# A one-core hybrid decoder layer: w_o's sums moved into the last branch, four transfers of x, and other orders on VectorE

## The chip, the cores and the metric

The kernel runs on one core of a Trainium2 chip. The engines that matter are TensorE (PE: matmuls and transposes, with PEld for its weight loads), VectorE (DVE), ScalarE (ACT), GpSimd (POOL) and SyncE (SP), whose queue issues nearly all DMAs. Each engine runs its own list of instructions in order and waits on semaphores for the others. The metric is device microseconds of one launch; 840.54 us before the change, the median of three runs (840.12 to 843.98).

## The reference

One layer, 512 rows of 1024 float32, batch 1:

```
u = rms_norm(x, mix_norm_g)
q, k, v, cf_val, cf_gate, sc_x, sc_bg, sc_cg, gates = split(u @ w_in)
q, k = rms_norm per head (8 heads of 64), then stick-breaking attention
y_a = o @ w_attn_out
y_b = silu(layer_norm(conv31(cf_val * sigmoid(cf_gate)) + b)) @ w_conf_out
y_c = (sc_bg * conv3(sc_cg * sc_x)) @ w_sc_out
merged = g0 * y_a + g1 * y_b + g2 * y_c          # g = sigmoid(gates + gate_b)
x = x + merged @ w_o
gt, up = split(rms_norm(x, ffn_norm_g) @ w_ffn_in)   # 2 x 2816 columns
x = x + (silu(gt) * up) @ w_ffn_out
```

## The kernel before, in words

**Numbers in two parts.** Each float32 operand of a matmul is split into a high part, rounded to the fast matmul type by ScalarE (L81), and a low part, the difference, which VectorE forms (L82). `mm3` (L89 to L91) multiplies high by high, high by low and low by high. `wsplit` splits a piece of a weight into tiles `wh` and `wl` (three buffers each); `unit` does one 128-column piece of a projection.

**Start.** `load_x` brings x in eight transfers of 256 KB. For each block of 128 rows ScalarE and VectorE each sum the squares of half a row (L284), one adds them (L286), ScalarE takes Ln and Exp, VectorE refines the inverse root (L291 to L293) and puts it on a diagonal (L295); TensorE then transposes and scales the block by 8 matmuls with that diagonal (L297). A block's squares are queued behind the block before. L304 and its ScalarE partner apply the norm's gain and split the result into `u`; the gains reach their layout by a transpose (L230).

**Stages.** Projections to the conformer gates, queries, keys and values; attention, with other projections between its steps (the query and key norms square a projection, split the square and average it by a matmul with `head_mean`); then the three branches, the last one of them `branch(1, ..., last=True)`, whose `product` multiplies a branch's result by its gate (L651) and adds it to `merged` (L652). Each pair of `merged` pieces becomes the operands of w_o in `quarters` (L559 to L562).

**Seven products.** w_o and w_ffn_out are multiplied in quarters, by seven products in place of eight. A product (j, p) is `seventh`: 6 matmuls on piece j of four (or of a few more in the FFN). Products 1, 6 and 7 come first, into banks p1, p6 and p7; for w_o their weights need b11 and the sums t3 = b22 - b12 (L791) and t2 = t3 + b11 (L792), made by `first_sums(j)`. `middle` then combines the banks: copies on ScalarE (L616 to L619), L615 and L620 on VectorE, the second L620 being `change`. Products 2 and 4 follow (their weights b21 and t2 - b21, L856), then 5 and 3 (t1 = b12 - b11, L871). Adds L862, L864, L884, L885 and L887 put the banks into the residual x1, and `turn` transposes x1 (L822) for the FFN between its matmuls. In `ffn_out` the last products' weights are likewise b21, b22 and the sums t1 and t4 (L954 to L956).

**What sets the order.** TensorE follows the order in which the program is written (`manual_schedule`); `queue` and `tick` interleave units with other work. The other engines are ordered by a scheduler that goes by priorities (`high_priority`, larger `offset` first) and by explicit `issue_after`. w_o's pieces come in seven transfers of 256 KB into `u` tiles, beside others into `raw` tiles, all in SyncE's queue.

## Time and profile before

| | |
|---|---|
| runs | 843.98, 840.54, 840.12 us |
| profiled execution | 839.71 us, its span 838.0 us |
| granted clock | 0.997 |
| TensorE / VectorE / ScalarE / GpSimd busy | 818.6 / 635.0 / 410.9 / 36.2 us |
| instructions in the span | 9783 |
| DMA | 90.13 MB, 108 GB/s on average |

The profile's times are of one execution, in microseconds from the start of its span. A matmul's record lasts longer than the step to the next one, since they are pipelined: what TensorE loses is read from starts. A wait's row names the engine that was waiting, the line and tile of its instruction, and what ended the wait last.

### The profile page before, as it was taken

What the parts mean: (1) busy time and instruction counts of PE and PEld (TensorE: products, weight loads), DVE (VectorE), ACT (ScalarE), POOL (GpSimd) and SP (SyncE); (2) the same over time, 40 slices, a digit from 0 to 9 for tenths busy, and PEclk for the clock granted to TensorE, in tenths of its full rate; (3) what the DMA queues carried; (4) which work ended last, traced back from release to release, by engine and by line L of the source; (5) the groups of instructions that cost most, each with busy time, mean ns of one, the idle gap of its engine ahead of it and who ended that gap; (6) DMA issues with size and microseconds to landing.
All of it is one profiled execution on the core that took longest, in us unless ns stands there. A gap on an engine that the chain in (4) does not pass through costs nothing.

```text
span 838.0 us, 9783 instructions
## 1 busy us (share of the span) xinstructions
PE 818.6 (98%) x3703; PEld 677.9 (81%) x3703; DVE 635.0 (76%) x952; ACT 410.9 (49%) x621; POOL 36.2 (4%) x60
## 2 busy tenths in 40 slices
PE   6999999999999999999998999999999999999997
PEld 6887887888888888888886778888888888888885
DVE  6598799897899999776578857555679865556796
ACT  6345698877664232573345554333345423333461
POOL 3100010002100000000000040000000000000000
PEclk9999999999999999999999999999999999999999
DMA  7333114112113143143241433332235733322452
GB/s 252 104 101 99 53 50 151 51 51 101 51 51 101 51 151 101 51 142 110 88 163 50 151 101 100 101 101 88 75 113 201 251 101 101 101 88 76 139 187 101
DMA packets 71468, 90.13 MB, mean 108 GB/s; under 512 B 2112, under 2 KB 56572, under 8 KB 71420
## 3 DMA queue, kind: packets, MB, share of 16 engines
q1 hardware_dynamic: 70252, 87.40, 31.3%
q10 hardware_dynamic: 1168, 2.10, 0.6%
q8 instruction: 29, 0.48, 0.2%
q14 instruction: 19, 0.16, 0.1%
HBM read 87.39 MB, written 2.10 MB: 107 GB/s over the span
## 4 chain that ended last, share of the span: by engine, by line
PE 89%; DVE 7%; issue 2%; ACT 1%; DMA 1%; SPq 0%; DVEq 0%; ACTq 0%
PE mm L90 75%; PE z L90 10%; PE o L90 3%; DVE wl L82 2%; DMA u<-in_w_o_dram 1%; ACT wh L81 1%; PE mm L297 1%; DVE cf L503 0%; DMA m<-in_x_dram 0%; PE z L297 0%; PE mm L822 0%; DVE tt L955 0%; DVE tt L956 0%; DVE tt L954 0%; DVE t L791 0%
## 5 line engine op out<-in xcount | busy, mean ns | idle before, releaser
L90 PE MATMUL mm<-u,wh 128*128 128x512 f32 x1536 | 474.9, 390 | 0.0
L90 PEld LDWEIGHTS mm<-u,wh 128*128 128x128 f32 x1536 | 287.2, 188 | 59.5 <-DVE u L304 0.6
L90 PE MATMUL mm<-u,wl 128*128 128x512 f32 x768 | 299.2, 390 | 0.0
L81 ACT CAST wh<-raw 128x1024 fp32r<-128x1024 f32 (+1 forms) x150 | 140.5, 937 | 240.5 <-PE mm L90 194.4
L82 DVE TENSOR_TENSOR wl<-raw,wh 128x1024 fp32r<-128x1024 f32 (+1 forms) x148 | 161.0, 1088 | 37.6 <-ACT wh L81 36.9
L90 PEld LDWEIGHTS mm<-u,wl 128*128 128x128 f32 x768 | 144.1, 188 | 30.1
L503 DVE SCALAR_TENSOR_TENSOR cf<-cf,cols_w,cf 128x512 f32<-128x512 f32 x120 | 89.8, 749 | 3.7 <-ACT cf L501 1.2
L916 DVE TENSOR_TENSOR t<-mm,cf 128x512 f32<-128x512 f32 x22 | 15.2, 691 | 59.7 <-PE mm L90 59.7
L90 PE MATMUL mm<-m,wh 128*128 128x512 f32 x128 | 39.4, 389 | 0.0
L81 ACT CAST wh<-tt 128x1024 fp32r<-128x1024 f32 x21 | 22.1, 1053 | 31.0 <-PE mm L90 16.5
L914 DVE TENSOR_TENSOR t<-mm,cf 128x512 f32<-128x512 f32 x22 | 15.1, 687 | 25.5 <-PE mm L90 25.4
L90 PE MATMUL mm<-wh,m 128*128 128x512 f32 x88 | 29.6, 392 | 0.0
L90 PEld LDWEIGHTS mm<-m,wh 128*128 128x128 f32 x128 | 24.0, 188 | 4.9
L82 DVE TENSOR_TENSOR wl<-tt,wh 128x1024 fp32r<-128x1024 f32 x21 | 25.6, 1220 | 2.9 <-ACT wh L81 2.8
L78 ACT ACTIVATE s<-s 128x384 f32<-128x384 f32 (+1 forms) x48 | 26.9, 561 | 1.1
L90 PE MATMUL z<-wh,m 128*128 128x512 f32 x72 | 26.0, 393 | 0.8 <-DVE z L620 0.8
L90 PE MATMUL mm<-m,wl 128*128 128x512 f32 x64 | 24.9, 389 | 0.0
L449 DVE SCALAR_TENSOR_TENSOR s<-z,s 128x384 f32<-128x384 f32 (+1 forms) x24 | 14.3, 598 | 11.6 <-ACT s L78 10.4
L834 POOL TENSOR_TENSOR cf<-cf,t 128x512 f32<-128x512 f32 x7 | 11.0, 1576 | 257.3 <-ACT t L832 257.1
L81 ACT CAST m<-t 128x512 fp32r<-128x512 f32 x21 | 13.1, 623 | 17.7 <-DVE t L560 11.3
L78 ACT ACTIVATE t<-t 128x512 f32<-128x512 f32 x31 | 19.6, 631 | 3.7 <-DVE t L914 3.6
L90 PEld LDWEIGHTS mm<-wh,m 128*128 128x128 f32 x88 | 16.8, 191 | 3.6
(301 smaller groups left out, 1135.6 us busy)
## 6 DMA issues: line engine op xcount, KB each, us to landing
raw<-in_w_in_dram SPq DMA_DIRECT2D x23, 1024.0 KB
raw<-in_w_ffn_in_dram SPq DMA_DIRECT2D x22, 1024.0 KB
raw<-in_w_ffn_out_dram SPq DMA_DIRECT2D x11, 1024.0 KB
raw<-in_w_ffn_out_dram SPq DMA_DIRECT2D x11, 512.0 KB
raw<-in_w_in_dram SPq DMA_DIRECT2D x10, 512.0 KB
raw<-in_w_ffn_out_dram SPq DMA_DIRECT2D x11, 256.0 KB
raw<-in_w_o_dram SPq DMA_DIRECT2D x9, 256.0 KB
m<-in_x_dram SPq DMA_DIRECT2D x8, 256.0 KB
```

The source lines that it names most:

```text
L78: table(nc.scalar.activation(o, i, f, **kw))
L81: (copy or nc.scalar.copy)(hi, src)
L82: return (sub or nc.vector.tensor_sub)(lo, src, hi.bitcast(F32))
L90: nc.tensor.matmul(o, lhsT, rhs, start=start, stop=stop, skip_group_check=True)
L297: nc.tensor.matmul(pts[f][:, t * P:(t + 1) * P], xblock(xt, t, f), diag, start=True, stop=True, skip_group_check=True)
L449: marks.append(nc.vector.scalar_tensor_tensor(t, z, 0.0, t, ALU.max, ALU.add))
L503: nc.vector.scalar_tensor_tensor(y, pad[:, n:n + S], w(n), y, ALU.mult, ALU.add)
L834: nc.gpsimd.tensor_add(sumsq, sumsq, s)
L914: nc.vector.tensor_mul(g, pg[0], rstd[0])
L916: nc.vector.tensor_mul(u, pu, rstd[0])
```

## The change

Line numbers L in this part are those of the changed file where the order of the change is quoted.

- x comes in four transfers of 512 KB, into tiles that the weights use later. The gains are transposed first, in another bank; 22 matmuls of the identity with itself follow on TensorE. The norm's steps are queued in a written order (`queued`): the squares of the next block stand between the sum of a block and its factor.
- In the norms of queries and keys the low part of the weight that is split third after (`low_after`) is queued behind the low part of the square.
- In the last branch the sums of w_o's pieces 0, 1 and 2 are called between its last units, those of piece 3 right behind; the last product's multiply is queued behind them.
- `middle` queues its changes one behind the other and its copies into p5 behind both. L900 (the former L856) stands behind `change` for all pieces. Products 2 and 4 of w_o are written as (0,2), (1,2), (0,4), (2,2), (1,4), (3,2), (2,4), (3,4); the t1 sums of three pieces stand ahead of the adds; the last adds have priority.
- In `ffn_out` sums t1 and t4 are formed each behind the last, and for the last two pieces ahead of the split of b21 and b22.

```diff
+WARM = 22
...
-    nsplit, queued_after, last_low = [0], {}, []
+    nsplit, queued_after, low_after = [0], {}, {}
 
     def wsplit(src):
         nsplit[0] += 1
@@ -145,8 +146,10 @@
             for ins in queued_after.get(nsplit[0], ()):
                 behind.enter_context(tc.issue_after(ins))
             hi, lo = alloc("wh", (P, kt, n), F32R), alloc("wl", (P, kt, n), F32R)
-            last_low[:] = [split_to(hi, lo, src,
-                                    sub=nc.gpsimd.tensor_sub if nsplit[0] in POOLW else None).ins]
+            nc.scalar.copy(hi, src)
+            if nsplit[0] in low_after:
+                behind.enter_context(tc.issue_after(low_after[nsplit[0]]))
+            (nc.gpsimd if nsplit[0] in POOLW else nc.vector).tensor_sub(lo, src, hi.bitcast(F32))
...
-    def load_x(tag):
+    def load_x(tags):
         t = []
-        for i in range(NT):
-            t.append([alloc(tag) for _ in range(2)])
-            for n in range(2):
-                nc.sync.dma_start(t[i][n], x[i * P:(i + 1) * P, n * S:(n + 1) * S])
+        for i, tag in enumerate(tags):
+            both = alloc(tag, (P, 2, S))
+            nc.sync.dma_start(both, x[i * P:(i + 1) * P, :].rearrange("p (n f) -> p n f", n=2))
+            t.append([both[:, n] for n in range(2)])
...
-        xt = load_x("m")
+        xt = load_x(("tt", "tt", "wh", "wl"))
...
-    transpose_rows(cols_g, rows_g, KT)
+    early = psum("o")
+    with tc.high_priority(offset=2000000):
+        transpose_rows(cols_g, rows_g, KT, "z")
+    for _ in range(WARM):
+        mm(early[:, :P], identr, identr, True, True)
...
+    chain = {}
+
+    def queued(engine, fn):
+        with ExitStack() as behind:
+            if engine in chain:
+                behind.enter_context(tc.issue_after(chain[engine].ins))
+            chain[engine] = fn()
+        return chain[engine]
+
+    sts = [cst.tile([P, 4], F32, name=f"st{t}") for t in range(NT)]
+    diags = [alloc("a", (P, P)) for _ in range(NT)]
+
+    def squares(t):
+        queued("act", lambda: nc.scalar.activation(
+            tmp(), xt[t][0], AF.Square, accum_out=sts[t][:, 0:1], scale=1.0 / 32))
+        queued("dve", lambda: nc.vector.scalar_tensor_tensor(
+            tmp(), xt[t][1], 1.0 / D, xt[t][1], ALU.mult, ALU.mult, accum_out=sts[t][:, 1:2]))
+
+    def power(t):
+        m, y = sts[t][:, 0:1], sts[t][:, 2:3]
+        queued("dve", lambda: nc.vector.scalar_tensor_tensor(m, m, EPS, sts[t][:, 1:2], ALU.add,
+                                                             ALU.add))
+        table(queued("act", lambda: nc.scalar.activation(y, m, AF.Ln)))
+        table(queued("act", lambda: nc.scalar.activation(y, y, AF.Exp, scale=-0.5)))
+
+    def factor(t):
+
+        m, y, a = sts[t][:, 0:1], sts[t][:, 2:3], sts[t][:, 3:4]
+        queued("dve", lambda: nc.vector.tensor_mul(a, y, y))
+        queued("dve", lambda: nc.vector.scalar_tensor_tensor(a, a, -0.5, m, ALU.mult, ALU.mult))
+        queued("dve", lambda: nc.vector.scalar_tensor_tensor(y, a, 1.5, y, ALU.add, ALU.mult))
+        queued("dve", lambda: nc.vector.tensor_scalar_mul(diags[t], ident, y))
+        for f in range(KT):
+            nc.tensor.matmul(pts[f][:, t * P:(t + 1) * P], xblock(xt, t, f), diags[t], start=True,
+                             stop=True, skip_group_check=True)
...
+        for step, t in ((squares, 0), (power, 0), (factor, 0), (squares, 1), (power, 1),
+                        (squares, 2), (factor, 1), (power, 2), (squares, 3), (factor, 2),
+                        (power, 3), (factor, 3)):
+            step(t)
+        before = [chain["act"].ins, chain["dve"].ins]
...
-                split_to(sh, sl, sq, nc.vector.tensor_copy)
+                nc.vector.tensor_copy(sh, sq)
+                low_after[nsplit[0] + 3] = nc.vector.tensor_sub(sl, sq, sh.bitcast(F32)).ins
...
+    def after(*ins):
+        stack = ExitStack()
+        stack.enter_context(tc.high_priority(offset=PRIO))
+        for i in ins:
+            stack.enter_context(tc.issue_after(i))
+        return stack
...
-                nc.scalar.copy(p5[i], s2[i])
+            behind = []
             for i in range(2):
                 s7.append(tmp())
-                nc.scalar.copy(s7[i], p7[i])
-                change = nc.vector.scalar_tensor_tensor(p7[i], p7[i], -1.0, s2[i], ALU.mult,
-                                                        ALU.subtract)
-        def rest():
-            for i in range(2):
-                nc.vector.tensor_add(x1_at(i + 2, 1), s7[i], x1_at(i + 2, 1))
+                copied = nc.scalar.copy(s7[i], p7[i])
+                with after(*behind):
+                    change = nc.vector.scalar_tensor_tensor(p7[i], p7[i], -1.0, s2[i], ALU.mult,
+                                                            ALU.subtract)
+                behind = [change.ins]
+            with after(copied.ins):
+                for i in range(2):
+                    nc.scalar.copy(p5[i], s2[i])
+
+        def rest(*behind):
+            with ExitStack() as stack:
+                for i in behind:
+                    stack.enter_context(tc.issue_after(i))
+                for i in range(2):
+                    nc.vector.tensor_add(x1_at(i + 2, 1), s7[i], x1_at(i + 2, 1))
+
         return p5, change.ins, rest
...
+                        if last and f == KT - 1:
+                            with after(*last_sum):
+                                nc.vector.tensor_mul(s[0], y, s[0])
+                            nc.vector.tensor_add(merged[f], merged[f], s[0])
+                        elif f not in merged:
...
-            t3, t2 = tmp(), alloc("c")
+            t3, t2 = alloc("cf"), alloc("c")
...
-    queue += units[:13] + [call(lambda: first_sums(0))] + units[13:]
+    queue += units[:13]
+    for j in range(3):
+        queue += [call(lambda j=j: first_sums(j)), units[13 + j]]
...
-        if j:
+        if j == n - 1:
...
+    fours = []
     for j in range(n):
-        with after(*[change][:j]):
+        with after(change):
             nc.vector.tensor_sub(t2s[j], t2s[j], b21[j])
         two, four = parts2(b21[j], t2s[j])
+        fours.append(four)
         seventh(mT[j][2], two, p1, False)
-        seventh(mT[j][4], four, p7, False)
-    with tc.high_priority(offset=PRIO):
+        for i in range(j - 1, j if j < n - 1 else n):
+            if i >= 0:
+                seventh(mT[i][4], fours[i], p7, False)
+    t1s, behind = [], []
+    for j in range(n - 1):
+        b11, b12, _ = wo_raw[j]
+        with after(*behind):
+            t1s.append(alloc("c"))
+            behind = [nc.vector.tensor_sub(t1s[j], b12, b11).ins]
+    with after(*behind):
...
-        with after(*[half][:j]):
-            t1 = alloc("c")
-            nc.vector.tensor_sub(t1, b12, b11)
-        held.append(parts2(b22, t1))
+        if j == n - 1:
+            with after(half):
+                t1s.append(alloc("c"))
+                nc.vector.tensor_sub(t1s[j], b12, b11)
+        held.append(parts2(b22, t1s[j]))
         if j == 1:
-            rest()
+            rest(half)
...
+    with tc.high_priority(offset=PRIO):
+        for i in range(2):
+            nc.vector.tensor_add(x1_at(i + 2, 1), x1_at(i + 2, 1), p5[i])
+            nc.vector.tensor_add(x1_at(i, 1), x1_at(i, 1), p5[i])
+        for i in range(2):
+            nc.vector.tensor_add(x1_at(i, 1), x1_at(i, 1), p3[i])
...
+        pieces, ws, formed = {}, [{} for _ in range(n)], []
+
+        def piece(j):
+            if j not in pieces:
                 with tc.high_priority():
                     w = alloc("raw", (P, 2, 2, S))
                     nc.sync.dma_start(w, w_ffn_out[(j0 + 2 * j) * P:(j0 + 2 * j + 2) * P].rearrange(
                         "(k p) (n f) -> p k n f", p=P, n=2))
-                pieces.append(w)
-                two, three = parts(w[:, 1], "u" if last and j == n - 1 else None)
-                ws.append({2: two, 3: three})
+                pieces[j] = w
+            return pieces[j]
+
+        def w23(j):
+            ws[j][2], ws[j][3] = parts(piece(j)[:, 1], "u" if last and j == n - 1 else None)
+
+        def w54(j):
+            (b11, b12), (b21, b22) = [[piece(j)[:, k, i] for i in range(2)] for k in range(2)]
+
+            def t14(t1, t4):
+                nc.vector.tensor_sub(t1, b12, b11)
+                nc.vector.tensor_sub(t4, b22, b21)
+                formed[:] = [nc.vector.tensor_sub(t4, t4, t1).ins]
+
+            behind = formed + [change][:j]
+            ws[j][5], ws[j][4] = parts(sums(t14, *behind),
+                                       "u" if last and j == n - 1 else None)
+
+        def go(*which):
+            for i, p in which:
+                seventh(h[i][p], ws[i][p], {2: p1, 3: p3, 4: p4, 5: p5}[p], p == 3 and i == 0)
+
+        ends = n - 2 if last else n
+        for j in range(ends):
+            w23(j)
             if j:
-                (b11, b12), (b21, b22) = [[pieces[j - 1][:, k, i] for i in range(2)]
-                                          for k in range(2)]
-                t1, t4 = parts(sums(t14, *[change][:j - 1]), "u" if last and j == n else None)
-                ws[j - 1].update({5: t1, 4: t4})
+                w54(j - 1)
             if j == 2:
-                rest()
-            now = [(j, p) for p in (2, 3) if j < ends] + [(j - 1, p) for p in (5, 4)
-                                                          if 0 < j <= ends]
-            if last and j == n:
-                now = [(i, p) for p in (5, 3, 4, 2) for i in (n - 2, n - 1)]
-            for i, p in now:
-                seventh(h[i][p], ws[i][p], {2: p1, 3: p3, 4: p4, 5: p5}[p], p == 3 and i == 0)
+                rest(change)
+            go((j, 2), (j, 3))
+            if j:
+                go((j - 1, 5), (j - 1, 4))
+        w54(ends - 1)
+        go((ends - 1, 5), (ends - 1, 4))
+        if last:
+            for fn in (w54, w23):
+                for j in (n - 2, n - 1):
+                    fn(j)
+            for p in (5, 3, 4, 2):
+                go((n - 2, p), (n - 1, p))
```

VectorE around the last product of the last branch; `t_3738` (before) and `t_3761` (changed) hold its gate, `raw` and `u` are pieces of w_o, `c` and `cf` or `t` their sums. Before:

```order
L792 TENSOR_TENSOR c_3678<-t_3677,raw_3673 128x512
...
L652 TENSOR_TENSOR v_2625<-v_2625,t_3671 128x512
L856 TENSOR_TENSOR c_3678<-c_3678,u_3936 128x512
L651 TENSOR_TENSOR t_3738<-mm_3744,t_3738 128x512
L652 TENSOR_TENSOR v_2625<-v_2625,t_3738 128x512
...
L791 TENSOR_TENSOR t_3800<-raw_3796 128x512
L562 TENSOR_TENSOR t_3760<-v_2625,t_3759 128x256
L792 TENSOR_TENSOR c_3801<-t_3800,raw_3796 128x512
L791 TENSOR_TENSOR t_3836<-raw_3832 128x512
```

And now:

```order
L832 TENSOR_TENSOR cf_3728<-raw_3724 128x512
L833 TENSOR_TENSOR c_3729<-cf_3728,raw_3724 128x512
...
L832 TENSOR_TENSOR cf_3767<-raw_3763 128x512
L833 TENSOR_TENSOR c_3768<-cf_3767,raw_3763 128x512
L832 TENSOR_TENSOR cf_3889<-u_3887,u_3885 128x512
L833 TENSOR_TENSOR c_3890<-cf_3889,u_3883 128x512
L83 TENSOR_TENSOR wl_3832<-c_3729,wh_3831 128x512
L83 TENSOR_TENSOR wl_3832<-cf_3728,wh_3831 128x512
L691 TENSOR_TENSOR t_3761<-mm_3775,t_3761 128x512
```

The sums of pieces 1, 2 and 3 have come ahead of the multiply, and the subtraction of piece 0's b21 (L856) is gone from here.

VectorE at a query norm in attention, before; `t_1183` is the square, `t_1185` its low part:

```order
L81 CAST t_1184<-t_1183 128x512
L82 TENSOR_TENSOR wl_1353<-raw_1033,wh_1352 128x1024
L82 TENSOR_TENSOR t_1185<-t_1183,t_1184 128x512
L449 SCALAR_TENSOR_TENSOR s_1204<-z_1200,s_1204 128x384
L81 CAST l_235_1209<-s_1204 128x384
```

And now:

```order
L378 CAST t_1199<-t_1198 128x512
L379 TENSOR_TENSOR t_1200<-t_1198,t_1199 128x512
L152 TENSOR_TENSOR wl_1368<-raw_1048,wh_1367 128x1024
L476 SCALAR_TENSOR_TENSOR s_1219<-z_1215,s_1219 128x384
L82 CAST l_232_1224<-s_1219 128x384
```

The low part of the square and that of the weight have changed places.

VectorE behind `middle` of w_o, now; the second L655 is `change`, `u` are the pieces b21, `wl_3961` holds the low parts for products (0,2) and (0,4):

```order
L655 SCALAR_TENSOR_TENSOR z_3819<-z_3819,t_3935 128x512
L83 TENSOR_TENSOR wl_3993<-u_3955,wh_3992 128x512
L655 SCALAR_TENSOR_TENSOR z_3820<-z_3820,t_3936 128x512
L900 TENSOR_TENSOR c_3693<-c_3693,u_3951 128x512
L900 TENSOR_TENSOR c_3729<-c_3729,u_3953 128x512
L900 TENSOR_TENSOR c_3768<-c_3768,u_3955 128x512
L83 TENSOR_TENSOR wl_3961<-c_3693,wh_3960 128x512
```

Before, piece 0's subtraction stood far ahead of this place (above), and only those of pieces 1 to 3 stood here; now piece 0's is the first of four behind `change`.

More of the change, by code (lines that the diff above doesn't have):

```diff
@@ L269, in hybrid_layer @@
     exp_log()
-    transpose_rows(cols_g, rows_g, KT)
+    early = psum("o")
[3 more added lines that the diff above has]
+        mm(early[:, :P], identr, identr, True, True)
     uT = [(alloc("u", dt=F32R), alloc("u", dt=F32R)) for _ in range(KT)]
     pts = [psum(tag) for tag in ["mm"] * 4 + ["z"] * 3 + ["o"]]
-    before = []
-    with tc.high_priority(offset=1000000):
-        for t in range(NT):
-            st = cst.tile([P, 4], F32, name=f"st{t}")
-            m, y, a = st[:, 0:1], st[:, 2:3], st[:, 3:4]
-            with ExitStack() as behind:
-                for ins in before:
-                    behind.enter_context(tc.issue_after(ins))
-                nc.scalar.activation(tmp(), xt[t][0], AF.Square, accum_out=m, scale=1.0 / 32)
-                nc.vector.scalar_tensor_tensor(tmp(), xt[t][1], 1.0 / D, xt[t][1], ALU.mult,
-                                               ALU.mult, accum_out=st[:, 1:2])
-            nc.vector.scalar_tensor_tensor(m, m, EPS, st[:, 1:2], ALU.add, ALU.add)
-            act(y, m, AF.Ln)
-            last = nc.scalar.activation(y, y, AF.Exp, scale=-0.5)
-            table(last)
-            nc.vector.tensor_mul(a, y, y)
-            nc.vector.scalar_tensor_tensor(a, a, -0.5, m, ALU.mult, ALU.mult)
-            nc.vector.scalar_tensor_tensor(y, a, 1.5, y, ALU.add, ALU.mult)
-            diag = alloc("a", (P, P))
-            before = [last.ins, nc.vector.tensor_scalar_mul(diag, ident, y).ins]
-            for f in range(KT):
-                nc.tensor.matmul(pts[f][:, t * P:(t + 1) * P], xblock(xt, t, f), diag, start=True,
-                                 stop=True, skip_group_check=True)
@@ L644, in product @@
                     def product(y, f=f, s=s):
-                        if f not in merged:
+                        if last and f == KT - 1:
[3 more added lines that the diff above has]
+                        elif f not in merged:
                             if f % 4 == 0:
@@ L770, in wo_piece @@
         return t
-    def after(*ins):
-        stack = ExitStack()
-        stack.enter_context(tc.high_priority())
-        for i in ins:
-            stack.enter_context(tc.issue_after(i))
-        return stack
     def first_sums(j):
@@ L951, in ffn_out @@
         p3, p4 = [psum("mm") for _ in range(2)], p7
-        def t14(t1, t4):
-            nc.vector.tensor_sub(t1, b12, b11)
-            nc.vector.tensor_sub(t4, b22, b21)
-            nc.vector.tensor_sub(t4, t4, t1)
-        ends = n - 2 if last else n
-        pieces, ws = [], []
-        for j in range(n + 1):
-            if j < n:
+        pieces, ws, formed = {}, [{} for _ in range(n)], []
+        def piece(j):
+            if j not in pieces:
                 with tc.high_priority():
```

11 lines of the change are left out of this document (3 added, 8 removed).

## The prediction

> **What bounds the kernel now.** I read the page's busy table and the chain first, then the waits of TensorE, then windows cut at the stages. The profiled execution took 839.71 us, 838.0 of it span; the median of the runs is 840.54.
>
> ```profile
> PE 818.6 (98%) x3703; PEld 677.9 (81%) x3703; DVE 635.0 (76%) x952; ACT 410.9 (49%) x621; POOL 36.2 (4%) x60
> PE 89%; DVE 7%; issue 2%; ACT 1%; DMA 1%; SPq 0%; DVEq 0%; ACTq 0%
> ```
>
> TensorE sets the end. No matmul is removed (22 are added), so only time in which TensorE stands still, or steps slowly, can be won. In the waits the columns are total, times, longest:
>
> ```profile
> PE mm L297 <- DVE a L295: 4.2, 1, 4.2
> PE o L230 <- POOL big_ident L221: 2.6, 1, 2.6
> PE z L90 <- DVE wl L82: 2.3, 3, 1.2
> PE mm L90 <- DVE wl L82: 1.8, 1, 1.8
> PE mm L90 <- DVE t L82: 1.4, 2, 1.1
> PE z L90 <- DVE z L620: 0.8, 1, 0.8
> PE mm L822 <- DVE v L887: 0.8, 1, 0.8
> PE z L90 <- ACT wh L81: 0.8, 1, 0.8
> PE mm L90 <- ACT wh L81: 0.7, 1, 0.7
> ```
>
> They name the places. What each costs I take from starts, since a matmul's record outlasts its step. Windows give span, TensorE busy with count, PEld, DVE, ACT, POOL, granted clock, DMA share, GB/s:
>
> ```profile
> 435.60:456.40 20.80, 18.33 (x73) 14.50 (x73) 18.21 (x32) 10.10 (x19) 0.00 (x0) 0.92 0.20 69
> 456.40:468.70 12.30, 11.46 (x49) 8.79 (x49) 10.43 (x19) 6.10 (x12) 0.00 (x0) 1.00 0.21 68
> 468.70:474.25 5.55, 4.39 (x19) 3.25 (x18) 5.55 (x11) 2.89 (x5) 0.00 (x0) 1.00 0.55 181
> 492.00:812.00 320.00, 320.00 (x1413) 264.90 (x1413) 215.21 (x307) 124.61 (x163) 4.32 (x3) 1.00 0.35 120
> 817.60:834.00 16.40, 14.53 (x61) 10.91 (x59) 12.47 (x19) 2.09 (x3) 0.00 (x0) 1.00 0.25 97
> 444.20:447.40 3.20, 3.20 (x8) 2.52 (x9) 2.10 (x5) 0.66 (x2) 0.00 (x0) 0.50 0.00 0
> ```
>
> From 492 to 812 TensorE never stops: 320/1413 = 0.2265 us a matmul is the fed step. In the others one of the count reaches in from before, so their own work is 72, 48, 18 and 60 matmuls, or 16.3, 10.9, 4.1 and 13.6 us; lost are 4.5, 1.4, 1.5 and 2.8 us. The last row adds that after a stop the step was 3.2/8 = 0.40 at a clock of 0.50.
>
> **The change part by part.**
>
> *A, the start.* Blocks of x follow one another (L284 to L295) on VectorE and ScalarE:
>
> ```profile
> 4.58 0.69 DVE L284 SCALAR_TENSOR_TENSOR t<-m 128x512 f32<-128x512 f32 x1 [4.58 <-DMA m<-in_x_dram]
> 6.05 0.16 DVE L291 TENSOR_TENSOR st<-st 128x1 f32<-128x1 f32 x1 [0.50 <-ACT st L288]
> 6.71 0.29 DVE L295 TENSOR_SCALAR a<-identr,st 128x128 f32<-128x128 f32 x1
> 13.72 0.29 DVE L295 TENSOR_SCALAR a<-identr,st 128x128 f32<-128x128 f32 x1
> 14.07 1.22 DVE L82 TENSOR_TENSOR wl<-raw,wh 128x1024 fp32r<-128x1024 f32 x1
> 15.30 2.07 DVE L304 SCALAR_TENSOR_TENSOR u<-mm,cols_g,u 128x512 fp32r<-128x512 f32 x3
> 7.05 2.08 PE L297 MATMUL mm<-a,m 128*128 128x128 f32 x8 [4.24 <-DVE a L295]
> 10.56 1.06 PE L297 MATMUL mm<-a,m 128*128 128x128 f32 x8
> 16.11 0.73 PE L90 MATMUL mm<-u,wh 128*128 128x512 f32 x2
> ```
>
> The four L295 are (13.72−6.71)/3 = 2.34 us apart, 0.5 of it VectorE's wait for ScalarE. Now the next block's square stands in that wait. VectorE's own work per block is about 0.65+0.2+0.2+3×0.2+0.25 = 1.9 us; four of them from 4.6, plus the waits that stay at both ends (2×0.5), reach 13.0 where it was 14.0. The weight's low part (14.07), the first L304 (15.30) and the first projection matmul (16.11) follow by 1.0 less. Fewer issues of x can at most bring the first square earlier, by some 0.4. Gain 1.0, at most 1.4. TensorE must keep up:
>
> ```profile
> 7.00:10.40 3.40, 3.35 (x15) 3.35 (x16) 2.58 (x11) 1.02 (x4) 2.10 (x9) 1.00 1.01 327
> 10.40:16.10 5.70, 5.70 (x51) 5.52 (x49) 4.32 (x14) 3.88 (x10) 0.00 (x0) 1.00 1.11 375
> ```
>
> Block 0 ran its 16 pieces at 3.4/16 = 0.21, the later ones at 5.7/51 = 0.11, although the clock's column says 1.00 in both. The 22 warm-up matmuls are put in its idle time before 7.05. If the first pieces stay at 0.21, the four blocks end at 10.4+3×1.8 = 15.8 and the gain is 0.3; if a stretch of the first projection also runs at 0.4, 3.2 us of it lose 1.6: low end −1.3.
>
> The Trainium skill, "TensorE: Matmul & The Clock Gate", Part 1, says in my words that the clock goes full after about 3.4 us of busy array and halves after about as much idleness. Block 0's 3.4 slow us agree; by that rule the warm-ups suffice if they fill 3.4 us, and the sum stays as it is; if they fill less, A is 0.3.
>
> *B, query norms.* The low part of a square stood behind a weight's (a window, then single instructions):
>
> ```profile
> 133.50:137.00 3.50, 2.35 (x10) 1.61 (x9) 3.40 (x7) 3.40 (x8) 0.00 (x0) 1.00 0.11 23
> 134.11 1.22 DVE L82 TENSOR_TENSOR wl<-raw,wh 128x1024 fp32r<-128x1024 f32 x1
> 135.25 0.68 DVE L82 TENSOR_TENSOR t<-t,t 128x512 fp32r<-128x512 f32 x1
> 135.98 0.50 PE L90 MATMUL mm<-t,head_mean 128*128 128x512 f32 x1 [1.15 <-DVE t L82]
> ```
>
> The two places cost the 1.4 of the waits' row, 1.1 and 0.3. Moved, the square ends a weight part earlier (1.14 here), and the weight 0.6 later; TensorE has queued matmuls of other units for microseconds in between. Gain 1.5 (1.2 to 1.6, with the clock's dent after each stop).
>
> *C, w_o's first products (435.6 to 456.4).*
>
> ```profile
> 435.51 0.69 DVE L856 TENSOR_TENSOR c<-c,u 128x512 f32<-128x512 f32 x1 [5.24 <-DMA u<-in_w_o_dram]
> 442.26 0.68 DVE L791 TENSOR_TENSOR t<-u,u 128x512 f32<-128x512 f32 x1
> 441.92 0.49 PE L90 MATMUL mm<-wh,s 128*128 128x512 f32 x1 [0.68 <-ACT wh L81]
> 444.20 0.79 PE L90 MATMUL mm<-wl,s 128*128 128x512 f32 x1 [1.79 <-DVE wl L82]
> ```
>
> VectorE stood 5.24 us on one L856 that is not needed before 456, with all of w_o's sums behind it. Then the pair j=1's parts came late, TensorE stopped at 441.9 and 444.2, and the next seven matmuls ran slowly: 4.5 in all. Now the sums of j=1, 2 and 3 stand ahead of the last product's multiply and L856 (now L900) behind `change`. Their 6×0.6 = 3.6 us fit into the 5.24; the parts of j=1 come at about 437.4 against a need at 441.1. All 4.5 can go. But the last multiply (L691) now stands behind j=3's sums, which wait for transfers 2 and 3 of the seven of w_o; transfer 4 was what L856 had at 435.5, and one more transfer of 256 KB stands ahead (0.8 us at the 327 GB/s of the start). L691 then goes at about 437.3, where it went at 436.1. That is just covered; each further microsecond costs one. All were there by 442.26 (L791 did not wait), so the bound is 5 us, plus 1.6 of slow clock. I take 4.0 (range 0 to 4.5).
>
> *D, 456.4 to 474.3.* Lost 1.4 (L620) and 1.5 (a low part at 473.0 behind adds). The changes are now chained and the t1 sums formed early: both go. But product (0,4) has come ahead of two others and needs c of L900, behind `change`:
>
> ```profile
> 457.06 0.70 DVE L620 SCALAR_TENSOR_TENSOR z<-z,t 128x512 f32<-128x512 f32 x1 [0.58 <-ACT t L619]
> 459.46 1.88 DVE L856 TENSOR_TENSOR c<-c,u 128x512 f32<-128x512 f32 x3
> ```
>
> From 457.06, L655, a low part, L655, three L900 and the low part are 7×0.6 = 4.2: ready at 461.3, while TensorE is through its two products and the next matmul at 459.4. So a wait of about 1.8 is new. Net gain 1.1 (0 if both changes also queue behind a copy; 2.9 if L900 overtakes).
>
> *E, the transposes at 486.*
>
> ```profile
> 484.44 1.45 DVE L82 TENSOR_TENSOR wl<-raw,wh 128x1024 fp32r<-128x1024 f32 x1
> 485.82 1.27 DVE L887 TENSOR_TENSOR v<-v,mm 128x512 f32<-128x512 f32 x2
> ```
>
> L887 now has priority over that 1.38 us. The stop was 0.8 to 1.0, with some 0.9 of slow transposes after it: gain 1.3 (0.7 to 1.9).
>
> *F, last output product.* Lost 2.8, the waits for low and high parts after 817.6 (the longest 1.2 among the three at z). The t1 and t4 sums now come a weight earlier; by VectorE's own durations (1.22 and 0.6) they are ready 2 us before their matmuls. A new wait of about 0.5 at the last piece's second part stays, since two plain adds and four more come ahead of it. Gain 2.2 (1.0 to 2.75).
>
> **Sum.** 1.0+1.5+4.0+1.1+1.3+2.2 = 11.1: 839.7−11.1 = 828.6 profiled; the median stood 0.8 above, so 829.4. All lows give −1.3+1.2+0+0+0.7+1.0 = 1.6, all highs 1.4+1.6+4.5+2.9+1.9+2.75 = 15.0 (825.5). The lows are not likely together; the range begins just short of all highs, and ends 1.4 above C at its low end alone (833.4), so that A at 0.3 and D at 0.4 may come with it: 834.8.
>
> **Rivals.**
>
> *Half of it comes back as new waits (0.17).* Each stop removed brings TensorE sooner to the next operand. Against it: after 492 nothing waits. For it: VectorE is busy 18.21 of 20.80 and 10.43 of 12.30 us there, so it has little to spare. With D at 0, C 2.5, F 1.0, A 0.3, and B and E as summed: 6.6 gained, 833.9.
>
> *VectorE blocked ahead of the last product (0.03, the other side).* L832 of j=3 waits for its transfers, L691 for it, TensorE for L691's quarters. It costs the landing time less 436, plus 1.6 of clock when the stop passes 2 us. The gain of the other parts and of C, 11.1, is used up at a landing of about 436+11.1−1.6 = 445.5; 0.5% slower (844.7) needs 450. Against: the same transfers were there by 442.26 and their buffers free in the same places. At 447 it would be 842.
>
> *Slow clock at the start (0.15).* Between the warm-ups and block 0, and between blocks, TensorE has gaps, of under 1 us between blocks and of up to 2 ahead of block 0. The stop of 1.15 at 135 left the clock at 1.00 (the window quoted under B), the double stop of 0.68 and 1.79 ahead of 444.2 brought it to 0.50. If it halves, A is −1.3: 831.7. The Trainium skill ("TensorE: Matmul & The Clock Gate", "What's actually happening") asks an idle window of about 3.4 us for the half clock, by which no gap here would do it and the time is 829.4; the trace disagrees, since shorter stops sufficed ahead of 444.2.
>
> *The orders don't do what they say (0.05).* If the start is set by the arrival of x and the sums of C wait for their transfers as before, only B, E and F stay: 5.0, 835.5.
>
> The rest, 0.60, is my forecast: 829.4, by itself 826 to 832. About 0.5% (4.2 us) is what a measurement of this kernel tells from no change. Faster by more (below 836.3) are forecast, first and third rival and nearly all of the last, 0.93; within, 0.05; slower, 0.02. The range 825.8 to 834.8 leaves out the two last rivals and the tails.
>
> **What would show it.** A: the first projection matmul at about 15.1 and clock 1.00 after 7. B: no wait of TensorE for a square's low part. C: no stop from 435 to 456, clock 1.00, the last multiply L691 at 437 to 438. D: one wait of 1 to 2 us at the third product after `change`, none at the t1 products. E: transposes without the 0.8. F: at most 0.5 before the last products. If L691 goes at 440 or later, C is wrong and the time lies above 831; a clock of 0.5 in the first 20 us means A is.

## The result, and the profile after

The changed kernel takes 831.46 us (median; 830.11 to 832.13) against 840.56 for the kernel before (840.12 to 843.98). The ratio is 0.9881, with a 95% interval of 0.9852 to 0.9910: 9.1 us faster, where the forecast was 11.1. The execution that was profiled took 832.13 us, 830.4 of it span, which is 7.6 less than the profiled execution before. Below I compare these two, part by part; a line number L in a row is that of the row's own kernel. The busy line of the changed kernel's page and the line of its chain:

```profile
PE 821.5 (99%) x3725; PEld 682.6 (82%) x3725; DVE 635.6 (77%) x952; ACT 411.3 (50%) x621; POOL 36.2 (4%) x60
PE 89%; DVE 7%; issue 2%; ACT 1%; DMA 1%; DVEq 0%; ACTq 0%
```

TensorE is still what sets the end. Its waits are now these (engine, line and tile waited for; total, times, longest):

```profile
PE z L233 <- DMA rows_g<-in_mix_norm_g_dram: 2.4, 1, 2.4
PE z L91 <- DVE wl L83: 0.7, 1, 0.7
PE mm L91 <- DVE u L870: 0.6, 1, 0.6
PE z L91 <- ACT wh L82: 0.6, 1, 0.6
PE mm L91 <- ACT t L875: 0.4, 1, 0.4
PE mm L91 <- DVE u L83: 0.3, 1, 0.3
```

Of the nine rows before, none is left as it was. Two rows are new in kind: `u L870` and `t L875`, the parts and squares of the transposed blocks ahead of the FFN. The windows of the three stages around w_o (span, TensorE busy with count, PEld, DVE, ACT, POOL, clock, DMA share, GB/s) are

```profile
435.35:452.10 16.75, 16.60 (x73) 13.41 (x72) 13.81 (x25) 8.87 (x17) 0.00 (x0) 1.00 0.23 75
452.12:468.86 16.74, 15.52 (x67) 12.26 (x66) 16.25 (x28) 9.43 (x18) 0.00 (x0) 1.00 0.33 111
468.88:483.55 14.67, 13.60 (x75) 10.94 (x74) 12.29 (x18) 9.18 (x14) 3.88 (x3) 1.00 0.36 123
```

The first products took 20.80 us before and take 16.75, which is the fed pace for 72 matmuls (16.3) and 0.4. The next stage, 66 matmuls, took 17.8 and takes 16.74. The third, from the first transpose to the last, was 14.46 long before and did not gain:

```profile
474.27:488.73 14.46, 13.58 (x75) 10.96 (x74) 10.98 (x15) 8.70 (x13) 4.99 (x3) 1.00 0.38 126
```

(That row is of the kernel before.) From such stretches, between the same instructions of both traces:

| part | stretch before | stretch after | change | forecast |
|---|---|---|---|---|
| A, up to the first projection matmul | 16.11 | 17.12 | +1.0 | -1.0 |
| B, from there to the first product of w_o | 419.5 | 418.2 | -1.3 | -1.5 |
| C, first products of w_o | 20.8 | 16.8 | -4.0 | -4.0 |
| D, to the first transpose | 17.8 | 16.8 | -1.1 | -1.1 |
| E, to the matmul behind the last transpose | 14.5 | 14.7 | +0.2 | -1.3 |
| F, from there to the last matmul | 345.0 | 342.9 | -2.1 | -2.2 |
| behind it | 4.3 | 4.0 | -0.3 | 0 |

Four of six terms came out as summed; A and E did not. A step, here and below, is the time from one matmul's start to the next one's. In A, TensorE's rows are

```profile
2.55 4.96 PE L91 MATMUL o<-identr 128*128 128x128 f32 x22
7.30 2.02 PE L316 MATMUL mm<-a,tt 128*128 128x128 f32 x8
10.82 1.83 PE L316 MATMUL mm<-a,tt 128*128 128x128 f32 x8
13.38 1.06 PE L316 MATMUL mm<-a,wh 128*128 128x128 f32 x8
15.17 1.06 PE L316 MATMUL mm<-a,wl 128*128 128x128 f32 x8
17.12 0.74 PE L91 MATMUL mm<-u,wh 128*128 128x512 f32 x2
```

and VectorE's factor of the last block, with the row behind it:

```profile
12.04 0.29 DVE L314 TENSOR_SCALAR a<-identr,st 128x128 f32<-128x128 f32 x1
12.39 1.22 DVE L152 TENSOR_TENSOR wl<-raw,wh 128x1024 fp32r<-128x1024 f32 x1
```

VectorE had the last factor at 12.3, 1.7 earlier than before and earlier than I had worked out. But block 3 started on TensorE only at 15.17: the rows of eight pieces last 2.0 and 1.8 us in blocks 0 and 1 and 1.06 in blocks 2 and 3, since the step fell from 0.21 to 0.11 only at 12.3. The warm-ups ran from 2.55 without a gap into block 0, and the step stayed 0.21 through them. The profile's clock column does not show this: it says 1.00 from 7.2 to 12.3 as well.

In E, VectorE's and TensorE's rows are

```profile
478.19 1.28 DVE L942 TENSOR_TENSOR v<-v,mm 128x512 f32<-128x512 f32 x2
479.38 1.23 DVE L152 TENSOR_TENSOR wl<-raw,wh 128x1024 fp32r<-128x1024 f32 x1
480.54 0.74 DVE L870 SCALAR_TENSOR_TENSOR u<-mm,cols,u 128x512 fp32r<-128x512 f32 x1
```

```profile
478.14 0.73 PE L91 MATMUL mm<-u,wh 128*128 128x512 f32 x2 [0.42 <-ACT t L875]
481.33 0.50 PE L91 MATMUL mm<-u,wh 128*128 128x512 f32 x1 [0.65 <-DVE u L870]
```

The adds L942 went ahead of the weight's low part, as the change says. L870 of block 3 went behind both. In the kernel before it (there L827) stood ahead of both, which began at 484.44 and 485.82:

```profile
483.57 0.74 DVE L827 SCALAR_TENSOR_TENSOR u<-mm,cols,u 128x512 fp32r<-128x512 f32 x1
```

So TensorE now reaches the last transposes without a stop, but it has stopped shortly before: at 478.14 for a square, and at 481.33 for L870.

### The profile page after: what moved, and what is told of

Read it like the earlier page. It is cut to its first block, busy times and chain, and to the rows that moved or that the text cites. A ratio compares the mean times of both kernels' runs of the same rounds, so it can differ in the third digit from the quotient of the medians.

```text
span 830.4 us, 9826 instructions
## 1 busy us (share of the span) xinstructions
PE 821.5 (99%) x3725; PEld 682.6 (82%) x3725; DVE 635.6 (77%) x952; ACT 411.3 (50%) x621; POOL 36.2 (4%) x60
## 4 chain that ended last, share of the span: by engine, by line
PE 89%; DVE 7%; issue 2%; ACT 1%; DMA 1%; DVEq 0%; ACTq 0%
PE mm L91 74%; PE z L91 10%; PE o L91 3%; DVE wl L152 1%; DMA u<-in_w_o_dram 1%; PE mm L316 1%; ACT wh L149 0%; PE z L316 0%; DVE wl L83 0%; DVE m L404 0%; PE mm L865 0%; DVE l L83 0%; DVE tt L1031 0%; DVE u L83 0%; DVE a L83 0%
## 5 line engine op out<-in xcount | busy, mean ns | idle before, releaser
L149 ACT CAST wh<-raw 128x1024 fp32r<-128x1024 f32 (+1 forms) x147 | 138.7, 944 | 234.2 <-PE mm L91 189.3
L152 DVE TENSOR_TENSOR wl<-raw,wh 128x1024 fp32r<-128x1024 f32 (+1 forms) x145 | 158.9, 1096 | 31.4 <-ACT wh L149 30.8
L82 ACT CAST m<-t 128x512 fp32r<-128x512 f32 x21 | 13.1, 623 | 17.8 <-DVE t L587 11.3
L91 PE MATMUL mm<-b,wh 128*128 128x512 f32 x64 | 19.7, 389 | 0.0
```

The costliest lines, as they stand in the source:

```text
L82: (copy or nc.scalar.copy)(hi, src)
L91: nc.tensor.matmul(o, lhsT, rhs, start=start, stop=stop, skip_group_check=True)
L149: nc.scalar.copy(hi, src)
L152: (nc.gpsimd if nsplit[0] in POOLW else nc.vector).tensor_sub(lo, src, hi.bitcast(F32))
```

## The experiments

The single times of the kernel before lay between 839.17 and 843.98 us over all, more scattered than those of the changed kernel (830.11 to 832.13). I therefore compare an edit of the changed kernel with the changed kernel's 831.4, which came again in the last group to 0.05 us, and give the ratio to the kernel before with its interval.

### The warm-ups

**None (warm0).**

```diff
-WARM = 22
+WARM = 0
```

> The changed kernel without its 22 warm-up matmuls. In the changed kernel every piece from 2.55 to 12.3 us stepped 0.21 us, warm-ups and blocks 0 and 1 of the norm alike, and the first projection matmul went at 17.12 (16.11 before the change). Theory 1, the warm-ups do not raise the clock: the norm's pieces are slow for 3.4 us or more from their own start at about 6.9, as they were before, the first projection matmul goes between 15 and 17, and the time is that of the changed kernel or up to 2 us less. Theory 2, they raise it but late: without them it is full later still, the first projection matmul goes after 17.5 and the time is 1 us longer or more.

831.26 us (831.00 to 831.43; ratio 0.9885, 0.9871 to 0.9900): no difference from the changed kernel.

```profile
7.03 2.08 PE L316 MATMUL mm<-a,tt 128*128 128x128 f32 x8 [3.35 <-DVE a L314]
10.60 1.59 PE L316 MATMUL mm<-a,tt 128*128 128x128 f32 x8
16.66 0.73 PE L91 MATMUL mm<-u,wh 128*128 128x512 f32 x2
```

This is theory 1: without them the step falls at 11.7, 4.6 us after block 0 began, and the first projection matmul goes at 16.66. The 22 warm-ups buy nothing that can be measured.

**In plain float32 (warm_f32), and on data of x (warm_x).**

```diff
-        mm(early[:, :P], identr, identr, True, True)
+        mm(early[:, :P], ident, ident, True, True)      # warm_f32
+        mm(early[:, :P], dense, ident, True, True)      # warm_x, dense = a corner of x
```

(What stands behind # in these cuts is for the reader and not in the kernels; ... marks lines left out.)

> The changed kernel with the 22 warm-ups in the number type of the norm's pieces (plain float32), still identity by identity. If the number type is why the clock stayed low, the step falls to 0.11 by about 7 us, the first projection matmul goes at about 15 and the time is 2 us below the changed kernel. If it is the data (nearly all zeros) or the warm-ups are too late in any case, the step stays 0.21 well past 9 us and the time is the same.

> The changed kernel with the 22 warm-ups in plain float32 on a 128 by 128 corner of x by identity, thus of the same form and kind of data as the norm's own pieces; the corner comes by a transfer of its own of 64 KB. If the zeros are why the clock stayed low, the step falls to 0.11 after 3.4 to 6.8 us of them, by 9.5 at the latest, the first projection matmul goes at 15 to 15.5 and the time is 1.5 to 2 us below the changed kernel. If data does not matter, it stays at about 17 as with the other warm-ups.

833.15 us (832.05 to 833.32; ratio 0.9905, 0.9890 to 0.9920) and 834.06 us (833.62 to 834.91; 0.9920, 0.9905 to 0.9935): both slower than the changed kernel, by 1.7 and 2.6. The rows of warm_f32, then of warm_x:

```profile
3.39 8.13 PE L91 MATMUL o<-identr 128*128 128x128 f32 x44
11.36 1.06 PE L316 MATMUL mm<-a,tt 128*128 128x128 f32 x8
```

```profile
4.93 6.96 PE L91 MATMUL o<-identr,dense 128*128 128x128 f32 x44
11.72 1.06 PE L318 MATMUL mm<-a,tt 128*128 128x128 f32 x8
```

Both expectations missed for a reason that I had not counted: in plain float32 the 22 matmuls are 44 records in the profile, at the same step, so they last 7 to 8 us and delay block 0 to 11.4 and 11.7. The clock did rise in them (the step fell to 0.11 after 6.1 us of the first and after 3.8 us of the second) and block 0 ran fast. So these two do not separate number type from data; they show that the clock can rise during warm-ups, and that their length is paid for once they run on past the time at which block 0 could begin.

**Wider ones, from the beginning (warm_dense).**

```diff
-WARM = 22
+WARM = 7
...
+    dense = alloc("m")[:, :2 * P]
+    nc.vector.memset(dense, 0.7)
+    early = psum("o")
+    for _ in range(WARM):
+        nc.tensor.matmul(early[:, :2 * P], dense[:, :P], dense, start=True, stop=True,
+                         skip_group_check=True)
...
-    for _ in range(WARM):
-        mm(early[:, :P], identr, identr, True, True)
```

> The changed kernel with other warm-ups: 7 plain float32 matmuls of 256 columns on a tile that VectorE fills with 0.7 at its start, ahead of the gains' transpose, about 6 us of TensorE at half clock from about 1 us on. Theory, the array takes the clock up once it has been busy for long enough before block 0: the step of the norm's pieces is 0.11 from the first one at 7, the first projection matmul goes at 14.4 to 15, and the time is 2 us below the changed kernel (829.5). Rival, the clock rises only after the norm itself has run for 3.4 us or more: 16 to 17, and the same time.

830.02 us (829.83 to 830.27; ratio 0.9866, 0.9843 to 0.9889), 1.4 below the changed kernel.

```profile
1.25 5.58 PE L199 MATMUL o<-m 128*128 128x256 f32 x14 [1.25 <-DVE m L196]
6.95 1.16 PE L319 MATMUL mm<-a,tt 128*128 128x128 f32 x8
9.81 1.16 PE L319 MATMUL mm<-a,tt 128*128 128x128 f32 x8 [0.81 <-DVE st L306]
15.44 0.73 PE L91 MATMUL mm<-u,wh 128*128 128x512 f32 x2
```

The clock was up before block 0: eight of its pieces took 1.16. TensorE then waited for block 1, and from 9.81 on three blocks follow one another at their own pace, 3 x 1.85 = 5.6 us, to 15.4. So even at full clock it is TensorE behind block 1's factor, not VectorE's last factor, that sets 15.4. That is 0.4 to 1.0 later than expected.

**The start of the kernel before (old_start).** The eight transfers, the old order of the norm and no warm-ups, in the changed kernel:

```diff
-        xt = load_x(("tt", "tt", "wh", "wl"))
+        xt = load_x("m")
...
-        for step, t in ((squares, 0), (power, 0), (factor, 0), (squares, 1), ...
+        for t in range(NT):                             # and on as before
...
```

> The changed kernel with the start of the kernel before: eight transfers of x, the squares of a block behind the factor of the block before, no warm-ups, the gains transposed where they were. Theory, the new start is worth nothing on average, because the norm's pieces run at half step longer there: the first projection matmul goes at 16.1 and the time is within 0.7 of the changed kernel's 831.5. Rival, the new start brings the 1.0 that I forecast and the look at 17.12 was an unlucky one: the time is 1 us above the changed kernel.

831.83 us (831.56 to 832.09; ratio 0.9887, 0.9868 to 0.9906), 0.4 above the changed kernel, and inside the scatter of the changed kernel's own times (830.11 to 832.13): the theory holds that the new start is worth next to nothing. Where the theory put the first projection matmul, at 16.1, it missed: it went at 17.16. The 16.11 of the kernel before was an early case. This table is read from TensorE's starts in the profiles, one execution each:

| start | kernel | step falls to 0.11 at | first projection matmul |
|---|---|---|---|
| as before | before | 10.4 | 16.11 |
| as before | wait_only | 10.7 | 17.05 |
| as before | old_start | 11.8 | 17.16 |
| as before | norms_and_ffn | 11.9 | 16.84 |
| changed | after | 12.3 | 17.12 |
| changed | turn_first | 9.6 | 15.75 |
| changed | sums_only | 11.5 | 17.16 |
| changed | after_again | 11.0 | 16.91 |
| changed, no warm-ups | warm0 | 11.7 | 16.66 |
| 7 wide warm-ups | warm_dense | about 6 | 15.44 |
| 7 wide warm-ups | best | about 6 | 15.63 |

The means of the last column are 16.79 for the start as before and 16.74 for the changed one.

**The changed kernel again (after_again).** Nothing edited.

> The changed kernel once more, with nothing edited, for the scatter of its start: the step of the norm's pieces falls to 0.11 at 12.31 in one execution and at 9.55 in another with the same start. Theory, the clock rises in steps of one window of about 3 us that does not follow the program: here again between 9 and 13, with the first projection matmul at 15.7 to 17.2 accordingly, every other stop in its place, and times that scatter over 2 us.

831.41 us (830.86 to 831.62; ratio 0.9881, 0.9864 to 0.9898). The stops at the other places were the same to 0.03 us. Only the small one at 445 was not there: w_o's transfer had landed earlier and the last multiply, L691, went at 436.74 in place of 437.86. The step fell at 11.0, and the first projection matmul went at 16.91. The five times scattered by 0.8, not by 2.

### The transposes (turn_first)

```diff
+        with tc.high_priority(offset=2 * PRIO):
             nc.scalar.activation(hi, pt, AF.Copy, scale=g)
             nc.vector.scalar_tensor_tensor(lo, pt, g, hi.bitcast(F32), ALU.mult, ALU.subtract)
...
-            nc.vector.tensor_add(x1_at(i, 1), x1_at(i, 1), p3[i])
+            added = nc.vector.tensor_add(x1_at(i, 1), x1_at(i, 1), p3[i])
+    low_after[nsplit[0] + 3] = added.ins
```

(and the same priority for the square)

> The changed kernel with the low part of each transposed block of x1 (L870), and its square on ScalarE, back in the order they had before the change, ahead of the last two adds L942; the adds stay ahead of the weight's low part. Theory, the gain at the transposes was lost because L870 of block 3 stands behind the adds and that weight: of the 2.1 us that TensorE lost from 477 to 486 in the changed kernel (at 478.1, 481.3 and 484.1) all but 0.5 go, and the time is 1.6 us below it. Rival, TensorE waits there for the next operand in any order, as VectorE has no room: the stop moves to the transposes again (0.8 to 1.9) and the time is the same within 0.5.

829.47 us (828.88 to 830.68; ratio 0.9869, 0.9850 to 0.9888), 2.0 below the changed kernel. Its waits:

```profile
PE z L233 <- DMA rows_g<-in_mix_norm_g_dram: 2.4, 1, 2.4
PE z L91 <- DVE wl L83: 0.7, 1, 0.7
PE z L91 <- ACT wh L82: 0.6, 1, 0.6
PE mm L91 <- DVE u L83: 0.3, 1, 0.3
PE mm L91 <- DVE u L871: 0.2, 1, 0.2
```

The row of the square is gone and that of `u` has fallen from 0.6 to 0.2. Stretch E of the table is 13.23 long here (467.06 to 480.29), 1.4 shorter than in the changed kernel and 1.2 shorter than in the kernel before; a stop of 0.5 stands right behind it. That is 1.4 of the 2.0; the other 0.6 is within the scatter of the four times. (The profiled execution also started 1.4 early, by chance.) The theory holds: the gain at the transposes was eaten by the new places of L870 and the square.

### What removed the stops of w_o's first products

**The wait alone (wait_only).** In the kernel before:

```diff
-        with after(*[change][:j]):
+        with after(change):
             nc.vector.tensor_sub(t2s[j], t2s[j], b21[j])
```

> The kernel before with one edit: the subtraction of w_o's first b21 (L856 for piece 0) stands behind `change` like the others, so that VectorE no longer waits 5.24 us for its transfer ahead of the last product; the sums of pieces 1 to 3 stay behind the last product's multiply. Theory 1, that wait is the cause of TensorE's stops at 441.9 and 444.2: they go, 4.5 us less, and a new wait of about 3 us comes at product (0,4), for a time of about 839. Theory 2, the sums' place in VectorE's order is the cause, since VectorE waits for the last product until 435.7 in any case: the stops stay within 0.6 us, the wait at (0,4) is added, and the time is 842 to 843.

847.45 us (846.15 to 848.07; ratio 1.0071, 1.0049 to 1.0093): slower, and by more than either theory said. VectorE, then TensorE:

```profile
436.95 0.69 DVE L651 TENSOR_TENSOR t<-mm,t 128x512 f32<-128x512 f32 x1 [5.63 <-PE mm L90]
```

```profile
442.76 0.51 PE L90 MATMUL mm<-wh,s 128*128 128x512 f32 x1 [0.48 <-ACT wh L81]
445.04 0.50 PE L90 MATMUL mm<-wl,s 128*128 128x512 f32 x1 [1.77 <-DVE wl L82]
460.22 0.50 PE L90 MATMUL z<-wh,m 128*128 128x512 f32 x1 [2.88 <-ACT wh L81]
461.98 0.80 PE L90 MATMUL z<-wl,m 128*128 128x512 f32 x1 [1.25 <-DVE wl L82]
```

VectorE's 5.24 us of waiting for a transfer became 5.63 of waiting for the last product; both of TensorE's stops stayed (0.6 and 2.05 from start to start), since the sums stand behind the multiply. That is theory 2. The time lies above its 842 to 843 mainly for two reasons. At (0,4), product 4 of piece 0, 4.6 us were lost, more than the 3 I had expected. And the next 13 steps were slow, which cost 2.8 more; eight slow steps came in the last output products too (1.6).

**The sums alone (sums_only).** In the changed kernel the first subtraction goes back ahead of the last multiply:

```diff
-        with after(change):
+        with after(*[change][:j]):
             nc.vector.tensor_sub(t2s[j], t2s[j], b21[j])
```

> The changed kernel with the subtraction of w_o's first b21 (L900 for piece 0) not held behind `change`: it stands right behind the sums and ahead of the last product's multiply, as it did before the change, and waits for its transfer there. Theory 2 of wait_only, the place of the sums is what removed the stops at 442 and 444: they stay away although VectorE waits for that transfer ahead of the multiply; the multiply goes up to 1.3 later and the small stop at 445.4 grows to at most 1.3; the 1.8 at (0,4) is gone: 0.5 to 1.5 us below the changed kernel. Theory 1, the wait itself mattered too: 2 us or more are lost again between 435 and 456.

829.89 us (829.66 to 830.36; ratio 0.9865, 0.9842 to 0.9887): 1.5 below the changed kernel.

```profile
434.06 0.69 DVE L832 TENSOR_TENSOR cf<-u,u 128x512 f32<-128x512 f32 x1 [2.10 <-DMA u<-in_w_o_dram]
436.60 0.68 DVE L900 TENSOR_TENSOR c<-c,u 128x512 f32<-128x512 f32 x1
437.20 0.68 DVE L691 TENSOR_TENSOR t<-mm,t 128x512 f32<-128x512 f32 x1
```

No stop of over 0.2 us was left from 435 to 468: neither those at 442 and 444, nor the 1.8 at (0,4). L900 did not even wait here, since by then the sum ahead of it (L832, 2.10) had waited for a transfer of the same batch. The two runs together show that the place of the sums removed the stops, and that holding the subtraction back behind `change` removed nothing and cost the 1.8 at (0,4). The sums were not moved alone in the kernel before; the tiles that they have now went with their place and were not tried apart.

### Two parts by themselves (norms_and_ffn)

The weight's low part behind the norms' squares, and the order of the output products, in the kernel before; the edits are those of the change.

> The kernel before with two parts of the change alone: the low part of weights behind the squares of the query and key norms (B), and the new order of the output products (F). By the traces of before and after, B takes the stops at 66.5 and 136 away but for 0.4 (1.5 us) and F those after 817.6 but for 0.6 (2.1 us), independent of the rest: 3.6 us below the kernel before. Rival, what they save depends on the other parts (the FFN's weights arrive with the same transfers, VectorE's order shifts): less than 2 us.

836.51 us (835.51 to 837.66; ratio 0.9943, 0.9926 to 0.9960): between 3.8 and 5.8 us below the kernel before by its medians in three groups (840.3, 842.35, 842.17), where 3.6 was expected. The stops left at these places are 0.6 (0.2 at 67 and 0.4 at 135) and 0.8 at 822, against 2.0 and 2.8 before: 3.4 of the 3.6, so the two parts do not depend on the rest. The trace also has w_o's first stops in full, but not what followed them. TensorE's rows, and the window behind them:

```profile
441.13 0.51 PE L90 MATMUL mm<-wh,s 128*128 128x512 f32 x1 [0.48 <-ACT wh L148]
443.41 0.50 PE L90 MATMUL mm<-wl,s 128*128 128x512 f32 x1 [1.77 <-DVE wl L151]
```

```profile
443.40:446.60 3.20, 3.19 (x14) 2.65 (x15) 3.17 (x6) 1.14 (x2) 0.00 (x0) 1.00 0.00 0
```

14 matmuls at a clock of 1.00, where the kernel before had 8 at 0.50 after the same stops. So of the 4.5 us that C lost before, 1.4 were a slow clock that comes in one execution and not in another; wait_only did not have it at this place either. The mean granted clock of single executions says the same of one and the same kernel. In this run it was 1.000 in the three that took 835.51, 835.93 and 836.23 us, and 0.997 or 0.998 in the three that took 836.79 to 837.66. In the 23 executions of the kernel before that ran in these groups it was 0.999 in the two fastest (839.17 and 839.3) and 0.996 or less in all above 841.7. All executions of the changed kernel had 1.000. So a part of the 9.1 us, which these records do not divide further, is clock that the kernel before lost in most of its executions.

### All repairs together (best)

```diff
+        low6 = low[0]                                   # low part of the first products' weights
...
-        with after(change):
+        with after(change if j else low6):
...
-            if j == 2:
+            if j == 2 and not last:
                 rest(change)
...
+            rest(low[0])                                # behind the last low parts
             for p in (5, 3, 4, 2):
```

with the edits of warm_dense and turn_first.

> The changed kernel with four repairs: the transposed blocks' order as in turn_first, the warm-ups as in warm_dense, piece 0's subtraction of b21 (L900) not behind `change` but behind the low parts of the first products, and the two plain adds of the last output product (L667) behind its last low parts. Theory, the stops that are left in the changed kernel are these and can be taken away one by one: the 1.8 at (0,4), the 0.6 at the last piece and 1.6 at the transposes go, the start gains 2, and the time is 831.5 - 6 = 825.5. Rival, VectorE is too busy around 450 and the wait goes elsewhere: at (0,4) or the t1 products 1 us or more is left, 827 or above; without the gain at the start 827.5.

826.55 us (825.76 to 826.80; ratio 0.9823, 0.9803 to 0.9842), 4.9 below the changed kernel where 6 was expected. The waits that TensorE still has:

```profile
PE o L201 <- DVE m L198: 1.2, 1, 1.2
PE mm L321 <- DVE st L308: 0.8, 1, 0.8
PE mm L93 <- DVE u L876: 0.2, 1, 0.2
```

The wait at (0,4) and that of the last output products are gone and did not come back elsewhere. What was missing from the 6 is the start, which gave 1.4 and not 2.0 (above), and the transposes, behind which 0.6 is still lost from start to start.

## Why the prediction was right or wrong

The sign, the range and the size (11.1 forecast, 9.1 measured) held; two of six terms did not, and one held with a wrong reason. The 2.0 between forecast and result is about what these two missed by: E by 1.5, and A by 0.6 if its worth is taken from old_start (0.4 in place of 1.0). That A misses by 2.0 in the table is in part chance: 16.11 is the earliest of the four old starts there, and 17.12 is among the latest of the new ones.

**A failed.** The step was "The 22 warm-up matmuls are put in its idle time before 7.05", used as if they raised the clock, with the sum then made along VectorE alone. VectorE's side was better than worked out: the last factor was there at 12.3, not 13.0. (The sum itself had a slip: 4.6, four times 1.9 and 1.0 make 13.2. VectorE began at 4.24, and a block came to about 1.8.) The sentence with the condition, "TensorE must keep up", was the one that decided. The step fell at 9.6 to 12.3 with these warm-ups, at 11.7 without them, and at 10.4 to 11.9 with the old start. I had the price of it (a gain of 0.3) and the rival (a loss of 1.3) and gave both too little. The new start is worth about 0.4 us by the medians (831.83 against 831.4) and 0.05 by the means of the table, and neither is clear of the scatter. Nor would the sum's reason have held with a full clock at 7, as warm_dense shows: from block 1's factor on TensorE goes by the blocks' own pace, and the first projection matmul goes at 15.4. That is 0.7 ahead of the 16.11 that I compared with, and 1.4 ahead of the old start's mean, 16.8. The Trainium skill, "TensorE: Matmul & The Clock Gate", "What's actually happening", says in my words that the window which watches the array runs freely and that the point of the change varies from run to run with it. The table above agrees that the point varies, but by more than the half microsecond either way that the Trainium skill states there: 9.6 to 12.3 with the same start. The figure of the Trainium skill, in the same section, of about 3.4 us of sustained work does not fit either: 22 narrow matmuls and the norm's pieces behind them, without a gap, left the step at 0.21 for 7.0 us in one execution (from 2.57) and for 9.8 in another (from 2.55). Counted from the first plain float32 record, the step fell after 3.4 to 4.9 us in the five starts without warm-ups, after 2.2 to 5.0 in the four with the 22 warm-ups of the fast type ahead, and after 3.8 and 6.1 in warm_x and warm_f32. That would suit warm-ups of the fast type counting for little. But whether number type, zeros or width was the reason is open: the two runs made for it differed in length as well.

**E failed.** The step was "L887 now has priority over that 1.38 us": true, but I did not ask what is late next on VectorE. The priority moved the adds ahead of L870 of block 3, and TensorE's matmuls behind the transposes need that one. It could have been read from the change's own order. turn_first gave back 1.4 in the trace: with L870 and the square in their old places E gains 1.2, close to the 1.3 of the sum.

**B, D and F held** to 0.2 us, D with its new wait of 1.8 at (0,4), which was 1.77 from start to start, and F with 0.6 left (the row `u L83` among the waits) where 0.5 was named.

**C held in size and not in reason.** I named two things, the sums' new place and the subtraction behind `change`; wait_only and sums_only show that the first did all of it and the second only caused D's new wait. The 4.0 also mixes 2.7 us of stops with 1.4 of a slow clock that not every execution has, so that its size is in part luck. The warning on the last multiply was right: it went at 437.86 behind the sum that waited for its transfers,

```profile
435.32 0.69 DVE L832 TENSOR_TENSOR cf<-u,u 128x512 f32<-128x512 f32 x1 [2.79 <-DMA u<-in_w_o_dram]
437.86 0.68 DVE L691 TENSOR_TENSOR t<-mm,t 128x512 f32<-128x512 f32 x1
```

0.6 later than worked out, and 0.4 us were lost for it at 445.4, about as priced. after_again, where it went at 436.74, lost nothing there.

**The rivals.** Half of the gain did not come back as new waits; 1.5 us did, at E. The block of VectorE ahead of the last product did not come. The slow clock at the start, which had 0.15, came in another way than this rival said: no gap halved the clock, it had never been full. Its time, 831.7, is the nearest to the 831.46 measured, but that is chance: the rival has A at a loss of 1.3, where old_start has it at a gain of about 0.4, and it leaves E's miss out.

## What to carry to other kernels

When an order is changed to bring one instruction forward, look at the two or three that it passes and at who waits for them; the gain is the difference, not the wait that goes. When two edits serve one wait, try each alone: here one did all and the other cost 1.5 us. A chain that is shortened on one engine is worth only what the next engine in it can follow, at the clock that this engine has there.

## What the runs showed that was not expected

- The clock at the start: TensorE busy from 2.55 without a gap stepped at 0.21 until 12.3 in one execution and until 9.6 in another; with 14 records of 256 columns (warm_dense, best) the step fell after 4.5 to 5 us. A warm-up has to be seen in the step of what follows it.
- The clock in mid-kernel: stops of about 0.6 and 2.05 us, one matmul apart, came with a clock of 0.50 in the kernel before and left it at 1.00 in wait_only and norms_and_ffn. Stops of 3.0 and 1.5, again one matmul apart, were followed by 13 slow steps in wait_only. No run shows what decides it.
- A plain float32 matmul of 128 columns makes two records, each of the 0.21 step that one record of the fast type has at that width and clock: 22 became 44.
- The first projection matmul varied by 1.05 us between four executions with the start of the kernel before (16.11 to 17.16), and by 1.41 between four with the changed start (15.75 to 17.16).
